# Weight sums of a seven-product down-projection: from loads and VectorE subtractions in the up-projection to accumulating DMAs beside the input projection

## The chip, the cores and the metric

The kernel runs on one core of a Trainium2 chip. The metric is the device time of one execution in microseconds (us). A profile is one execution of its own; its time is given beside the median of the timed runs.

## The reference

One hybrid decoder layer on 1024 tokens of width 1024, with 16 learned meta tokens put ahead (1040 rows in all). The input projection feeds four differential-attention heads and four HGRN2 heads side by side; their outputs are joined, projected and added to the residual; a gated FFN with a causal convolution of width 3 follows.

```python
a = rmsnorm(h, ln_mix_pre)
dq, dk, dv, hq, hf, hi, hg = split(a @ w_in)
mix = concat([diff_attention(dq, dk, dv, ...), hgrn2(hq, hf, hi, hg, ...)]) @ w_out
h = h + rmsnorm(mix, ln_mix_post)
a = rmsnorm(h, ln_ffn_pre)
u = causal_depthwise_conv(a @ w_up, conv_w, 3) + conv_b      # 1024 -> 2 x 2816
gate, up = split(u, 2)
y = (gelu(gate) * up) @ w_down                               # 2816 -> 1024
h = h + rmsnorm(y, ln_ffn_post)
return h[16:]
```

All inputs and outputs are float32.

## The kernel before

**Products.** Each float32 operand is split into a high part (a cast on ScalarE) and a low part (a subtraction on VectorE or POOL), both fp32r; each product is three matmuls (high by high, high by low, low by high). `split` does it, and `load_split` loads a tile first (SP issues nearly all DMAs).

**Input projection and heads.** `dense()` yields the projection of one tile of 128 columns after the other, each in three groups of rows (`proj_group`); while a tile is being multiplied the next one's weights are loaded and split. `interleave` mixes its steps with those of a head: the tiles of HGRN head h with attention head h, the tiles of attention head h+1 with HGRN head h. The loop over the four heads runs 25 tiles, 75 groups, through `dense`. Ahead of it, the attention's bias tables are made: `rb` tiles, partly cleared by POOL, are stored to DRAM (`rsc<-rb`). The first HGRN head's `f`, written by ScalarE, later takes over the place of the `rb` tiles. In each HGRN head POOL helps with products over halves of a tile (`tt<-t`).

**FFN up-projection.** The width of 2816 is cut into 22 blocks of 128 (`ft`), for gate and up side each. Both FFN projections use a seven-product scheme in place of eight (a Strassen type), in which sums of operand quarters are multiplied. Block 0 is done plainly (`plain_unit`); for each later block, `prep` makes seven split weight operands (`uh`, `ul`, from loads `ra` and sums `ws`), and `unit(ft, p)`, for the two halves p of the rows, does the seven products into three PSUM banks `pa`, `pb`, `pc`. Copies and additions between products write `x1` (`x<-pa`), `u2`, `u3` (`u<-pb,x`), and the outputs `ug`, `uu`. The fourth and the sixth product are added into `pb` again, so they have to wait until VectorE has read it. `gated` then does the convolution (`c`), gelu and product, and stores to the DRAM tensor `gsc`.

**Down-projection.** Its seven-product scheme needs four sums of quarters of the weight matrix, 1408 x 512 each. Before, `down_sums` in the up-projection makes them from block 6 (`SUMS`) on, at four of the seven steps of a block: per row tile k of 11, SP loads the four quarters into SBUF (`wd`, in the four "gk" buffers of the pool "down"), VectorE subtracts four times (`wd<-wd,wd`, 128 x 512), and SP stores the results to the DRAM tensor `tsc`. The tail then runs the products in `ORDER` 1, 2, 5, 6, 3, 7, 4, each over 11 row tiles: `operands` loads the gated activations (`gi<-gsc`, in "gk" buffers too, or the kept `ga`, `gb`, `gc`, `gs`) and the weights (`wi`, from `w_down` or `tsc`) and splits both into `gh`, `gl` and `wh`, `wl`; the matmuls go into `pd`.

**Order.** TensorE's instructions stand in the order in which the program is written. VectorE, ScalarE, POOL and SP get an order from the scheduler, which looks at when an instruction's inputs and its buffer are ready by its own costs; each engine then runs its list strictly in order, and so does SP with its DMAs. `issue_after` holds an instruction until another has been issued. All elementwise instructions pass through one helper, line 54.

Of the kernel before, what the change touches and what calls it, by code (L numbers as in the profile page):

```python
# [9 lines left out]
F32 = mybir.dt.float32  # L10
# [3 lines left out]
ALU = mybir.AluOpType  # L14
# [3 lines left out]
P = 128  # L18
# [6 lines left out]
NF = DFF // P  # L25
# [6 lines left out]
WN = [258, 256]  # L32
C0 = [0, 514]
FA, FH, FO = 840, 800, 740
SUMS = 6


def start(i):
# [21 lines left out]
def interleave(dense, sides, fill, lead=0):  # L60
    sides = list(sides)
    live = True

    def feed(budget):
        nonlocal live
        while live and budget > 0:
            c = next(dense, False)
            if c is False:
                live = False
            elif c is None:  # L70
                return
            else:
                budget -= c

    feed(lead)
    while sides:
        for s in list(sides):
            c = next(s, False)
            if c is False:
                sides.remove(s)  # L80
                continue
            feed(fill * (c or 1))
    feed(1e12)
# [3 lines left out]
def layer_kernel(ctx: ExitStack, tc: tile.TileContext, x, meta, table, lbl, gpre, gpost, win,  # L87
# [3 lines left out]
    V, A = Ordered(tc, nc.vector, state), Ordered(tc, nc.scalar, state)  # L91
    G = Ordered(tc, nc.gpsimd, state)
    T, SY = nc.tensor, nc.sync

    def pool(name, bufs, side="left", space=None):
        kw = {"side": side} if space is None else {"space": space}
        cm = tc.tile_pool(name=name, bufs=bufs, reuse_waits="tile", **kw)
        return cm, cm.__enter__()
# [35 lines left out]
    tsc = dp.tile([4, DFF // 2, 512], F32, tag="tsc", name="tsc")  # L134
# [47 lines left out]

    last_load = []

    at_p_cm, ap_ = pool("attn", 1, "right")
    z_cm, zp = pool("pre", 2, "right")

# [3 lines left out]
    def proj_group(g, parts, name, evac):  # L191
        b0, b1 = GROUPS[g]
        t0, t1 = start(b0), start(b1 - 1) + P
        n = t1 - t0
        pt = ps_in(f"pi_{name}_{g}")
        for k in range(KD):
            yield from proj_step(pt[:, :n], parts, k, t0, t1, lambda: evac(g, b0, b1, t0, t1, pt[:, :n]))
# [14 lines left out]
    gb = zp.tile([P, D], F32, tag="gb", name="gb", bufs=1)  # L212
# [121 lines left out]
    def carried():  # L334
        tails = list(carry)
        carry.clear()
        return tails
# [385 lines left out]
                yield from values(i + 1)  # L723
        carry.append(pend.pop("tail"))

    def dense(tiles, preload=None):
        parts = preload
        for idx, (m, name, evac) in enumerate(tiles):
            if parts is None:
                parts = load_m(m, name)  # L730
            nxt = load_m(tiles[idx + 1][0], tiles[idx + 1][1]) if idx + 1 < len(tiles) else None
            for g in range(3):
                for step, c in enumerate(proj_group(g, parts, name, evac)):
                    if step == 14:
                        flush()
                    yield c
            parts = nxt

    t_a, tiles = attn_in(0)
# [188 lines left out]

    for h in range(HEADS):
        t_h, tiles_h = hgrn_in(h)  # L930
        interleave(dense(tiles_h), [attn(h, t_a)] + carried(), FA, 1500)
        if h < HEADS - 1:
            t_a, tiles_a = attn_in(h + 1)
            interleave(dense(tiles_a), [hgrn_head(t_h)] + carried(), FH, 1500)

    close(at_cm)
    wo_cm, wop = pool("wo", 7)
# [283 lines left out]
    for i in range(1, NBLK):  # L1221
        py = ps_b(f"py1_{i}")
# [42 lines left out]
    marks = {}  # L1265
# [100 lines left out]
    dn_cm, dn = pool("down", 4, "right")  # L1366
    next(p0)
    for j in range(4, 7):
        prep(7 + j)

    def down_sums():
        for k in range(NF // 2):
            b = {}
            for nm, kk, half in (("11", k, 0), ("12", k, 1), ("22", k + NF // 2, 1), ("21", k + NF // 2, 0)):
                b[nm] = dn.tile([P, 512], F32, tag="gk", name=f"wd{nm}_{k}")
                SY.dma_start(b[nm], wdown[P * kk: P * (kk + 1), 512 * half: 512 * (half + 1)])
            yield
            for j, d, p_, q_ in ((0, "11", "12", "11"), (2, "12", "22", "12"), (1, "22", "22", "11"), (3, "21", "21", "22")):
                V.tensor_tensor(b[d], b[p_], b[q_], op=ALU.subtract)
                SY.dma_start(tsc[j][P * k: P * (k + 1)], b[d])  # L1380
                yield

    wd_sums = down_sums()
    for ft in range(1, NF):
        units = [unit(ft, p, ps_b) for p in range(2)]
        for j in range(7):
            prep(7 * (ft + 1) + j)
            for u in units:
                next(u)
            if ft >= SUMS and j in (1, 3, 5, 6):  # L1390
                with tc.issue_after(marks["last"].ins):
                    next(wd_sums, None)
            if (ft, j) == (1, 1):
                with tc.issue_after(marks[1, 1].ins):
                    next(p1)
# [31 lines left out]
    def sums5(k):  # L1427
        SY.dma_start(keep["gc"][:, k], g_src(k, 1))
        b = g_in(k + NH, 1, "5")
        V.tensor_tensor(keep["gs"][:, k], keep["gc"][:, k], b, op=ALU.add)  # L1430
        SY.dma_start(keep["ga"][:, k], g_src(k, 0))

    def operands(pr, k):
        ga, gb, gc, gs = (keep[nm][:, k] for nm in ("ga", "gb", "gc", "gs"))
        if pr == 1:
            a = g_in(k, 0, "1")
        elif pr == 2:
            SY.dma_start(gb, g_src(k + NH, 0))
            a = gb
        elif pr == 5:  # L1440
            a = gs
        elif pr == 6:
            V.tensor_tensor(gs, gs, ga, op=ALU.subtract)
            a = gs
        elif pr == 3:
            V.tensor_tensor(gb, gb, gs, op=ALU.subtract)
            a = gb
        elif pr == 7:
            V.tensor_tensor(ga, ga, gc, op=ALU.subtract)
            a = ga  # L1450
        else:
            a = g_in(k + NH, 1, "4")
        b = w_in(pr, k)
        nm = f"{pr}_{k}"
        gh = dn.tile([P, 512], F32R, tag="gh", name=f"gh{nm}")
        gl = dn.tile([P, 512], F32R, tag="gl", name=f"gl{nm}")
        split(gh, gl, a, V)
        wh = wp.tile([P, 512], F32R, tag="wh", name=f"wh{nm}", bufs=4)
        wl = wp.tile([P, 512], F32R, tag="wl", name=f"wl{nm}", bufs=4)
        split(wh, wl, b, V)  # L1460
        return gh, gl, wh, wl
# [41 lines left out]
    def evac(pr, m, py):  # L1503
        if pr == 1:
            A.copy(x1[:, m], py)
        elif pr == 2:
            V.tensor_tensor(c11[:, m], py, x1[:, m], op=ALU.add)
            squares(c11[:, m], m, 0)
            as_bias(m, 0)
            G.tensor_tensor(c11[:, m], c11[:, m], gfo[:, :512], op=ALU.mult)  # L1510
        elif pr == 5:
            A.copy(x5[:, m], py)
        elif pr == 6:
            V.tensor_tensor(u2[:, m], py, x1[:, m], op=ALU.add)
        elif pr == 3:
            c = u2[:, m]
            V.tensor_tensor(c, py, c, op=ALU.add)
            squares(c, m, 1)
            s_ = rstd(m, 1)
            hh = fp.tile([P, D], F32, tag="hh", name=f"hh{m}", bufs=2)  # L1520
            SY.dma_start(hh, hsc[P * m: P * (m + 1), :])
            V.scalar_tensor_tensor(hh[:, :512], c11[:, m], s_, hh[:, :512], ALU.mult, ALU.add)
            G.tensor_tensor(c, c, gfo[:, 512:], op=ALU.mult)
            V.scalar_tensor_tensor(hh[:, 512:], c, s_, hh[:, 512:], ALU.mult, ALU.add)
            SY.dma_start(out[P * m: P * (m + 1), :], hh)
        elif pr == 7:
            V.tensor_tensor(x1[:, m], py, x1[:, m], op=ALU.add)
            c = x5[:, m]
            V.tensor_tensor(c, c, x1[:, m], op=ALU.add)
            squares(c, 4 + m, 1)  # L1530
            as_bias(4 + m, 1)
            G.tensor_tensor(c, c, gfo[:, 512:], op=ALU.mult)
        else:
            c = x1[:, m]
            V.tensor_tensor(c, py, c, op=ALU.add)
            squares(c, 4 + m, 0)
            V.tensor_tensor(c, c, gfo[:, :512], op=ALU.mult)
            s_ = rstd(4 + m, 0)
            hh = hhs[m]
            V.scalar_tensor_tensor(hh[:, :512], c, s_, hh[:, :512], ALU.mult, ALU.add)  # L1540
            if m == 3:
                V.scalar_tensor_tensor(hh[:, 512:], x5[:, m], s_, hh[:, 512:], ALU.mult, ALU.add)
            else:
                A.mul(x5[:, m], x5[:, m], s_)
                G.tensor_tensor(hh[:, 512:], hh[:, 512:], x5[:, m], op=ALU.add)
            SY.dma_start(out[P * (4 + m): P * (5 + m), :], hh)
# [91 lines left out]
```

## Time and profile before

| | |
|---|---|
| median of three runs | 1334.59 us (1334.57 to 1335.59) |
| profiled execution | 1334.41 us |
| its span | 1332.6 us |
| mean granted TensorE clock | 0.995 |
| TensorE busy | 1288.0 us, 97% |
| VectorE, ScalarE, POOL busy | 931.6, 692.5, 456.2 us |
| DMA engines, mean busy share | 38%, 165 MB |
| FFN up-projection, blocks 2 to 21 | 694.6 to 1106.1 us |

In the profile, PE is TensorE, PEld its weight loads, DVE is VectorE, ACT ScalarE, POOL GpSimd and SP SyncE, whose queue issues the DMAs. A row of the timeline gives start, duration, engine, line, operation, output and inputs, shapes, and in brackets how long the engine stood before it and for what. A row of a group gives count, busy time in us and the mean of one in ns, then the idle time before. A row of the waits gives the waiting and the awaited instruction, then us in total, times, and the longest. A row cut by windows gives the stretch, its length, and the busy time and count of PE, PEld, DVE, ACT and POOL, then the granted clock, the DMA share and GB/s. A row of the DMA issues gives count, KB each, and the median time to landing.

### The profile page before, as it was taken

Reading aid. Unit: us, or ns where it says so; the run is one execution under the profiler, and the core shown is the slowest. Engines: PE = TensorE matmul, PEld = TensorE weight load, DVE = VectorE, ACT = ScalarE, POOL = GpSimd, SP = SyncE. Lnnn points to the kernel's source line nnn. Section 1 sums busy time; section 2 is a strip of 40 time slices with the busy share of each in tenths; the row PEclk is TensorE's granted clock in tenths of the full one; section 3 lists DMA queues with packets and bytes.
Section 4 is the critical chain, followed back from the end, with each engine's and each line's share of the span. In section 5 each row is a group of like instructions: output and inputs, shape, how many; then the busy total and the mean of one; then the engine's idle time right before and its main releaser. Section 6 shows DMA issues by size and latency. Waiting matters only on the chain.

```text
span 1332.6 us, 26191 instructions
## 1 busy us (share of the span) xinstructions
PE 1288.0 (97%) x10172; PEld 1187.6 (89%) x10172; DVE 931.6 (70%) x1531; ACT 692.5 (52%) x1635; POOL 456.2 (34%) x340
## 2 busy tenths in 40 slices
PE   8999999999999999899999999999999989999997
PEld 7899999899999988677999999999999988878875
DVE  6464646465645664547997788988989886697586
ACT  8465466447544755246754444444444444454553
POOL 5211211121112110344076667677676630010121
PEclk9999999999999999999999999999999999999999
DMA  6111111112111234587232224545445436955363
GB/s 208 61 41 32 54 56 41 48 45 64 44 41 33 88 100 152 170 265 265 83 111 80 80 96 152 181 147 163 162 147 170 156 120 214 329 176 166 88 205 119
DMA packets 99427, 165.00 MB, mean 124 GB/s; under 512 B 10035, under 2 KB 34899, under 8 KB 99302
## 3 DMA queue, kind: packets, MB, share of 16 engines
q1 hardware_dynamic: 99302, 163.32, 37.8%
q8 instruction: 80, 1.31, 0.4%
q14 instruction: 45, 0.37, 0.1%
HBM read 122.65 MB, written 40.63 MB: 123 GB/s over the span
## 4 chain that ended last, share of the span: by engine, by line
PE 43%; DVE 10%; DMA 4%; issue 3%; ACT 3%; POOL 1%; SPq 0%; DVEq 0%; ACTq 0%; POOLq 0%
PE pd L1484 5%; PE pd L1483 5%; PE pd L1485 5%; PE pb L1316 4%; DVE c L54 3%; PE pb L1317 3%; PE pb L1318 3%; PE pa L1316 2%; PE pa L1317 2%; PE pa L1318 2%; PE pc L1316 2%; PE pc L1317 2%; PE pc L1318 2%; DMA gi<-gsc 1%; DVE ul L54 1%
## 5 line engine op out<-in xcount | busy, mean ns | idle before, releaser
L1316 PE MATMUL pb<-t,uh 128*128 128x258 f32 x504 | 144.8, 287 | 11.9 <-DVE u L54 11.8
L1317 PE MATMUL pb<-t,uh 128*128 128x258 f32 x504 | 142.3, 282 | 0.0
L1318 PE MATMUL pb<-t,ul 128*128 128x258 f32 x504 | 142.3, 282 | 0.0
L1484 PE MATMUL pd<-wl,gh 128*128 128x512 f32 x308 | 122.0, 396 | 0.5 <-DVE wl L54 0.5
L1483 PE MATMUL pd<-wh,gh 128*128 128x512 f32 x308 | 121.7, 395 | 0.0
L1485 PE MATMUL pd<-wh,gl 128*128 128x512 f32 x308 | 121.7, 395 | 0.0
L54 POOL TENSOR_TENSOR c<-c,c 128x514 f32<-128x514 f32 (+1 forms) x44 | 74.9, 1702 | 120.6 <-ACT c L54 110.3
L1316 PEld LDWEIGHTS pb<-t,uh 128*128 128x128 f32 x504 | 96.1, 191 | 15.2 <-DVE u L54 15.0
L54 DVE SCALAR_TENSOR_TENSOR c<-uu,cwt,c 128x514 f32<-128x514 f32 (+1 forms) x88 | 87.6, 1004 | 22.6 <-ACT c L54 22.3
L1317 PEld LDWEIGHTS pb<-t,uh 128*128 128x128 f32 x504 | 96.3, 191 | 0.0
L1318 PEld LDWEIGHTS pb<-t,ul 128*128 128x128 f32 x504 | 95.9, 190 | 0.0
L1316 PE MATMUL pa<-t,uh 128*128 128x258 f32 (+1 forms) x336 | 95.2, 283 | 0.0
L1318 PE MATMUL pa<-t,ul 128*128 128x258 f32 (+1 forms) x336 | 95.0, 283 | 0.0
L1317 PE MATMUL pa<-t,uh 128*128 128x258 f32 (+1 forms) x336 | 94.8, 282 | 0.0
L1316 PE MATMUL pc<-t,uh 128*128 128x258 f32 (+1 forms) x336 | 94.4, 281 | 0.0
L1317 PE MATMUL pc<-t,uh 128*128 128x258 f32 (+1 forms) x336 | 94.0, 280 | 0.0
L1318 PE MATMUL pc<-t,ul 128*128 128x258 f32 (+1 forms) x336 | 93.7, 279 | 0.0
L54 DVE SCALAR_TENSOR_TENSOR c<-ug,cwt,c 128x514 f32<-128x514 f32 (+1 forms) x88 | 88.2, 1002 | 1.5 <-ACT c L54 1.4
L54 ACT CAST uh<-ra 128x512 fp32r<-128x512 f32 x67 | 41.0, 616 | 67.9 <-PE pb L1317 49.7
L54 POOL TENSOR_TENSOR ul<-ws,uh 128x512 fp32r<-128x512 f32 x42 | 63.8, 1519 | 27.1 <-ACT uh L54 27.1
L1484 PEld LDWEIGHTS pd<-wl,gh 128*128 128x128 f32 x308 | 57.7, 187 | 15.8 <-DVE wl L54 1.9
L1483 PEld LDWEIGHTS pd<-wh,gh 128*128 128x128 f32 x308 | 57.7, 187 | 14.1
(373 smaller groups left out, 4169.5 us busy)
## 6 DMA issues: line engine op xcount, KB each, us to landing
ra<-in_wup_dram SPq DMA_DIRECT2D x88, 256.0 KB, 3.0
mp<-msc SPq DMA_DIRECT2D x23, 512.0 KB, 5.5
wd<-in_wdown_dram SPq DMA_DIRECT2D x44, 256.0 KB, 3.3
tsc<-wd SPq DMA_DIRECT2D x44, 256.0 KB, 3.1
wi<-tsc SPq DMA_DIRECT2D x44, 256.0 KB, 2.8
gi<-gsc SPq DMA_DIRECT2D x33, 256.0 KB, 3.6
wi<-in_wdown_dram SPq DMA_DIRECT2D x33, 256.0 KB, 4.2
gsc<-c SPq DMA_DIRECT2D x22, 257.0 KB, 2.3
```

The source lines that it names most:

```text
L54: ins = call(*args, **kw)
L1316: T.matmul(pt, hi[:, s], th[:, k], start=(first and k == 0), stop=False, skip_group_check=True)
L1317: T.matmul(pt, hi[:, s], tl[:, k], start=False, stop=False, skip_group_check=True)
L1318: T.matmul(pt, lo[:, s], th[:, k], start=False, stop=(k == 3), skip_group_check=True)
L1483: T.matmul(py, gh[:, s], wh, start=(k == 0 and pr not in (3, 7)), stop=False, skip_group_check=True)
L1484: T.matmul(py, gh[:, s], wl, start=False, stop=False, skip_group_check=True)
L1485: T.matmul(py, gl[:, s], wh, start=False, stop=(k == NH - 1), skip_group_check=True)
```

## The change

The four weight sums are made wholly in DRAM. `down_sums` now sits ahead of the head loop and is a generator that `dense` advances once per projection group, for 55 steps. Per row tile k, SP copies four quarters of `w_down` into the four parts of `tsc`, DRAM to DRAM; then POOL issues four DMAs that add into these: parts 0 and 2 get a second quarter, part 3 gets part 1 (one row tile later), part 1 gets part 0. The adds are cut into pieces of 512 bytes, 128 elements each, by `max_dma_last_dim=512`. `issue_after` ties both to the latest weight load. [...] The loads, subtractions, stores and the `SUMS` of the up-projection are gone. In the scheduled order of the changed kernel TensorE's list is the same as before; the `gi` loads of the tail's first four row tiles, with their `gh` and `gl`, stand in blocks 1 to 4 of the up-projection, where they stood in the last blocks before.

```diff
--- before.py
+++ after.py
@@ -32,7 +32,6 @@
 WN = [258, 256]
 C0 = [0, 514]
 FA, FH, FO = 840, 800, 740
-SUMS = 6
 
 
 def start(i):
@@ -182,6 +181,33 @@
 
     last_load = []
 
+    def down_sums():
+        def quarter_of(k, r, c):
+            kk = k + NF // 2 * r
+            return wdown[P * kk: P * (kk + 1), 512 * c: 512 * (c + 1)]
+
+        def add(j, k, src):
+            with tc.issue_after(last_load[-1].ins):
+                G.dma_start(tsc[j][P * k: P * (k + 1)], src, accum_op=ALU.add, max_dma_last_dim=512)
+
+        for k in range(NF // 2 + 1):
+            if k < NF // 2:
+                for j, r, c in ((0, 0, 1), (2, 1, 1), (1, 1, 1), (3, 1, 0)):
+                    with tc.issue_after(last_load[-1].ins):
+                        SY.dma_start(tsc[j][P * k: P * (k + 1)], quarter_of(k, r, c))
+                yield
+                add(0, k, quarter_of(k, 0, 0))
+                yield
+                add(2, k, quarter_of(k, 0, 1))
+                yield
+            if k:
+                add(3, k - 1, tsc[1][P * (k - 1): P * k])
+                yield
+            if k < NF // 2:
+                add(1, k, tsc[0][P * k: P * (k + 1)])
+                yield
+
+    wd_sums = down_sums()
     at_p_cm, ap_ = pool("attn", 1, "right")
     z_cm, zp = pool("pre", 2, "right")
 
@@ -723,13 +749,14 @@
                 yield from values(i + 1)
         carry.append(pend.pop("tail"))
 
-    def dense(tiles, preload=None):
+    def dense(tiles, preload=None, side=iter(())):
         parts = preload
         for idx, (m, name, evac) in enumerate(tiles):
             if parts is None:
                 parts = load_m(m, name)
             nxt = load_m(tiles[idx + 1][0], tiles[idx + 1][1]) if idx + 1 < len(tiles) else None
             for g in range(3):
+                next(side, None)
                 for step, c in enumerate(proj_group(g, parts, name, evac)):
                     if step == 14:
                         flush()
@@ -928,10 +955,10 @@
 
     for h in range(HEADS):
         t_h, tiles_h = hgrn_in(h)
-        interleave(dense(tiles_h), [attn(h, t_a)] + carried(), FA, 1500)
+        interleave(dense(tiles_h, None, wd_sums), [attn(h, t_a)] + carried(), FA, 1500)
         if h < HEADS - 1:
             t_a, tiles_a = attn_in(h + 1)
-            interleave(dense(tiles_a), [hgrn_head(t_h)] + carried(), FH, 1500)
+            interleave(dense(tiles_a, None, wd_sums), [hgrn_head(t_h)] + carried(), FH, 1500)
 
     close(at_cm)
     wo_cm, wop = pool("wo", 7)
@@ -1367,29 +1394,12 @@
     next(p0)
     for j in range(4, 7):
         prep(7 + j)
-
-    def down_sums():
-        for k in range(NF // 2):
-            b = {}
-            for nm, kk, half in (("11", k, 0), ("12", k, 1), ("22", k + NF // 2, 1), ("21", k + NF // 2, 0)):
-                b[nm] = dn.tile([P, 512], F32, tag="gk", name=f"wd{nm}_{k}")
-                SY.dma_start(b[nm], wdown[P * kk: P * (kk + 1), 512 * half: 512 * (half + 1)])
-            yield
-            for j, d, p_, q_ in ((0, "11", "12", "11"), (2, "12", "22", "12"), (1, "22", "22", "11"), (3, "21", "21", "22")):
-                V.tensor_tensor(b[d], b[p_], b[q_], op=ALU.subtract)
-                SY.dma_start(tsc[j][P * k: P * (k + 1)], b[d])
-                yield
-
-    wd_sums = down_sums()
     for ft in range(1, NF):
         units = [unit(ft, p, ps_b) for p in range(2)]
         for j in range(7):
             prep(7 * (ft + 1) + j)
             for u in units:
                 next(u)
-            if ft >= SUMS and j in (1, 3, 5, 6):
-                with tc.issue_after(marks["last"].ins):
-                    next(wd_sums, None)
             if (ft, j) == (1, 1):
                 with tc.issue_after(marks[1, 1].ins):
                     next(p1)
@@ -1427,7 +1437,7 @@
     def sums5(k):
         SY.dma_start(keep["gc"][:, k], g_src(k, 1))
         b = g_in(k + NH, 1, "5")
-        V.tensor_tensor(keep["gs"][:, k], keep["gc"][:, k], b, op=ALU.add)
+        V.tensor_tensor(keep["gs"][:, k], b, keep["gc"][:, k], op=ALU.subtract)
         SY.dma_start(keep["ga"][:, k], g_src(k, 0))
 
     def operands(pr, k):
@@ -1440,13 +1450,13 @@
         elif pr == 5:
             a = gs
         elif pr == 6:
-            V.tensor_tensor(gs, gs, ga, op=ALU.subtract)
+            V.tensor_tensor(gs, gs, ga, op=ALU.add)
             a = gs
         elif pr == 3:
-            V.tensor_tensor(gb, gb, gs, op=ALU.subtract)
+            V.tensor_tensor(gb, gs, gb, op=ALU.subtract)
             a = gb
         elif pr == 7:
-            V.tensor_tensor(ga, ga, gc, op=ALU.subtract)
+            V.tensor_tensor(ga, gc, ga, op=ALU.subtract)
             a = ga
         else:
             a = g_in(k + NH, 1, "4")
...
         elif pr == 6:
-            V.tensor_tensor(u2[:, m], py, x1[:, m], op=ALU.add)
+            V.tensor_tensor(u2[:, m], py, x1[:, m], op=ALU.subtract)
         elif pr == 3:
             c = u2[:, m]
-            V.tensor_tensor(c, py, c, op=ALU.add)
+            V.tensor_tensor(c, c, py, op=ALU.subtract)
...
         elif pr == 7:
-            V.tensor_tensor(x1[:, m], py, x1[:, m], op=ALU.add)
+            V.tensor_tensor(x1[:, m], py, x1[:, m], op=ALU.subtract)
             c = x5[:, m]
-            V.tensor_tensor(c, c, x1[:, m], op=ALU.add)
+            V.tensor_tensor(c, x1[:, m], c, op=ALU.subtract)
...
             c = x1[:, m]
-            V.tensor_tensor(c, py, c, op=ALU.add)
+            V.tensor_tensor(c, py, c, op=ALU.subtract)
```

## The prediction

> **What bounds the kernel now.** I read the page's shares first, then the chain that ended last, then what TensorE waited for.
>
> ```profile
> span 1332.6 us, 26191 instructions
> PE 1288.0 (97%) x10172; PEld 1187.6 (89%) x10172; DVE 931.6 (70%) x1531; ACT 692.5 (52%) x1635; POOL 456.2 (34%) x340
> ...
> PE 43%; DVE 10%; DMA 4%; issue 3%; ACT 3%; POOL 1%; SPq 0%; DVEq 0%; ACTq 0%; POOLq 0%
> ...
> PE pb L1316 <- DVE u L54: 9.3, 11, 3.5
> ```
>
> TensorE is busy for 97% of the span, and the change does not touch its instructions, so the most that can be won is the 3% in which it stands, and what it loses to a slow clock. The last row is TensorE's waits from 770 to 1110 us, the FFN's up-projection with the sums: 9.3 us in 11 waits for one thing, VectorE's read of the `pb` bank (`u2`, `u3`) before the next product may be added into it. To see what the sums cost I cut the up-projection at the start of a block (`x<-pa`): blocks 2 to 6 without sums, 7 to 18 with them, 19 to 21 and the rest of block 21.
>
> ```profile
> core 0: us, PE busy (x) PEld busy (x) DVE busy (x) ACT busy (x) POOL busy (x), PEclk, DMA share, GB/s
> 694.58:794.03 99.45, 99.45 (x839) 99.36 (x838) 76.05 (x113) 48.00 (x87) 64.78 (x45) 1.00 0.25 83
> 794.03:1042.24 248.21, 242.36 (x2017) 240.00 (x2017) 222.10 (x304) 113.45 (x206) 173.84 (x108) 1.00 0.49 159
> 1042.24:1106.09 63.85, 60.34 (x492) 59.83 (x491) 49.19 (x75) 28.48 (x52) 25.62 (x17) 0.97 0.39 127
> ...
> L54 DVE TENSOR_TENSOR wd<-wd,wd 128x512 f32<-128x512 f32 x44 | 51.1, 1161 | 0.0
> ```
>
> In the first stretch TensorE has no gap (99.45 of 99.45) and a block takes 99.45/5 = 19.89 us. In the second VectorE is busy for 222.10 of 248.21 us (89%, against 76% before) and a block takes 248.21/12 = 20.68 us; its 44 subtractions `wd` (mean 1161 ns) are the main thing that the first stretch lacks.
>
> **Part 1: the sums leave the up-projection.** Removed: 44 loads, 44 subtractions, 44 stores. What matters on the path is the excess of the second and third stretch over the free pace. Blocks 7 to 18: 248.21 − 12 × 19.89 = 9.5 us. Blocks 19 to 21 have 492 TensorE instructions, of 2017/12 = 168 a block, so 2.93 blocks: 63.85 − 2.93 × 19.89 = 5.6 us. Sum **−15.1**. The instructions of block 7 on then stand on VectorE in the order that blocks 4 and 5 have now, and these have no gap, so nothing else is late next. The floor of this term is −9.3 (the waits alone), the ceiling −15.1 and what a smaller DMA load might add. The 88 issues that SP loses pay nothing, as SP is idle between them.
>
> **Part 2: what moves in their place.** The tail's operands for its first product (`gi`, split into `gh` on ScalarE and `gl` on VectorE) use the same "gk" buffers as the `wd` tiles. With these gone the buffers are free from the start: the instruction order of the changed kernel has `gi_0` to `gi_3` behind the `gsc` stores of blocks 0 to 3, and `gh`, `gl` of each in the middle of blocks 1 to 4, instead of blocks 19 and 20. What such a move does is already seen once, at the tail:
>
> ```profile
> 1053.01 0.32 SPq L1415 DMA_DIRECT2D gi<-gsc  x1
> ...
> 1056.38 0.62 ACT L54 CAST gh<-gi 128x512 fp32r<-128x512 f32 x1 [3.45 <-DMA gi<-gsc]
> ...
> 1072.84 1.72 DVE L54 TENSOR_TENSOR gl<-gi,gh 128x512 fp32r<-128x512 f32 x1
> ...
> 1072.97 0.39 PE L1316 MATMUL pb<-t,uh 128*128 128x258 f32 x1 [3.47 <-DVE u L54]
> ...
> 1074.10:1077.30 3.20, 3.20 (x16) 3.08 (x16) 3.20 (x4) 0.00 (x0) 3.12 (x2) 0.50 0.60 189
> ```
>
> An engine that reaches such a copy stands until the load has landed (3.45 us on ScalarE, with a load issued 3.35 us earlier). And after TensorE's gap of 3.47 us its granted clock is 0.50 over the whole of 1074.10 to 1077.30: 16 matmuls where the full clock would have done some 32, so about 1.7 us lost beside the gap. Block 1 now:
>
> ```profile
> 687.40 0.33 SPq L1284 DMA_DIRECT2D gsc<-c  x1
> 699.50 2.91 SPq L1284 DMA_DIRECT2D gsc<-c  x2
> 718.96 2.91 SPq L1284 DMA_DIRECT2D gsc<-c  x2
> 739.35 2.92 SPq L1284 DMA_DIRECT2D gsc<-c  x2
> ...
> 687.73 1.44 DVE L54 TENSOR_TENSOR ul<-ra,uh 128x512 fp32r<-128x512 f32 x1
> 689.09 0.41 DVE L54 TENSOR_TENSOR uu<-pb,x 128x258 f32<-128x258 f32 x1
> 690.45 0.76 DVE L54 SCALAR_TENSOR_TENSOR c<-uu,cwt,c 128x514 f32<-128x514 f32 x1 [0.95 <-ACT c L54]
> 696.97 0.69 DVE L54 TENSOR_TENSOR ul<-ra,uh 128x512 fp32r<-128x512 f32 x1
> 700.55 0.74 DVE L54 TENSOR_TENSOR u<-pb,x 128x258 f32<-128x258 f32 x2
> ...
> 701.02 0.39 PE L1316 MATMUL pb<-t,uh 128*128 128x258 f32 x1
> ```
>
> Block 0's last store is issued at 687.40 to 687.73; `gi_0` goes out right behind and lands some 3.1 us later, at 690.9. `gh_0` (0.62) ends at 691.5, `gl_0` (0.69, as the `ul` at 696.97, which has the same shape) at 692.1, and the `ul` that now starts at 687.73 follows, so `uu_0` starts at 692.75 instead of 689.09: VectorE is late by 3.65 us. From there to 700.55 it runs all but without a pause (one wait of 0.95, for ScalarE's copy of that same `uu`), so `u2` of block 2, at 700.55, and the matmul behind it, at 701.02, are 3.65 late: **+3.65**, and, as the gap is as long as that of 3.47, a half-clock spell of **+1.7**. In blocks 2 to 4 `gl_k` stands ahead of `u3_0`, which product 5 waits for. By the second store of each pair (issued at the end of its row), a load of 3.1 and 0.62 for `gh`, between 0.69 and 1.57 for `gl`, and 0.41 for `u3`, that is ready at about 727.0 in block 3 and 747.4 in block 4, some 0.3 and 0.7 us behind TensorE's present pace; in block 2 TensorE is late already: **+1.0**. Sum +6.35. Bounds: +3, if the stall of block 1 falls under 2.5 us and no spell follows; +18, if each of blocks 2 to 4 stands for 2.5 us and has a spell too (5.35 + 3 × 4.2).
>
> **Part 3: the DMAs beside the input projection.** Added: 44 copies DRAM to DRAM on SP and 44 accumulating DMAs issued by POOL, one step ahead of each of the first 55 projection groups. POOL takes its instructions in order: the second row's add waits until the first row's add has landed, and the add of the third row until the second's, so POOL stands at these. Behind them stand the last `rb` memset and the halving trees.
>
> ```profile
> 56.67 0.21 POOL L54 MEMSET rb<- 128x128 f32 x1 [0.25 <-DVE rb L54]
> 58.10 0.33 SPq L308 DMA_DIRECT2D rsc<-rb  x1
> 65.19 0.43 ACT L54 ACTIVATE f<-kr 128x272 f32<-128x272 f32 x1
> 147.14 0.40 POOL L54 TENSOR_TENSOR tt<-t 128x130 f32<-128x130 f32 x1 [11.38 <-DVE hq L54]
> 152.11 0.70 DVE L54 TENSOR_TENSOR kr<-kr,tt 128x520 f32<-128x520 f32 x1
> ...
> wr_hi<-in_win_dram SPq DMA_DIRECT2D x8, 256.0 KB, 2.6
> X_in<-in_win_dram SPq DMA_DIRECT2D x3, 256.0 KB, 7.3
> rsc<-rb SPq DMA_DIRECT2D x4, 192.0 KB, 2.5
> ```
>
> `f` takes over the place of `rb` in SBUF and so waits for the last `rsc` store. To keep 65.19 the memset must start by 65.19 − 2.5 − 0.21 = 62.5. The first add can go at about 52, when its copy is there. With L from an add's start to its landing and c for POOL's own time per issue, the memset comes free at 52 + 2L + c. No row of before shows either. For L I take a load, a store and an issue, 2.6 + 2.5 + 0.33 ≈ 5.5 (bounds: 2.6, one transfer alone, and 7.3 + 2.5 ≈ 10). For c I take four times SP's 0.33, as the rows are cut into four pieces, 1.3 (bounds 0.33, and 4, three POOL passes of 1.3 us). `f` is then late by 2 × 5.5 + 1.3 − 10.5 = 1.8 us; as TensorE has little slack there I count 1.5 of it. The trees have 152.11 − 147.5 = 4.6 us of slack, and POOL is free for 11.4 us ahead of them, which four issues of 1.3 do not fill: 0. For 44 issues on SP's queue and the traffic 0.5. Sum **+2.0** (0 to +16).
>
> By the Trainium skill's page "DMA: Bandwidth & Descriptors", section "Anatomy of one DMA — SWDGE (gpsimd) path", a DMA issued by GpSimd takes 2.0 us and its bytes by 436e3, by which I estimate 2.6 us for 262,144 bytes. By that `f` is not late, and the sum would be 1.5 us lower. No run here shows it.
>
> **Part 4: turned signs.** The tail's subtractions and sums are as many, on the same engine, with the same operands: 0.
>
> **Sum.** −15.1 + 6.35 + 2.0 = −6.75 on the profiled execution's own 1334.41 us (span 1332.6; the median of the three is 1334.59, 0.2 above), so **1327.7 us**. A difference of 0.2%, 2.7 us, is about what a measurement of this kernel can tell from none.
>
> **Rivals.**
> *The waits of the moved split are hidden.* If `gi_0` lands within 1 us of need, part 2 is +1 and part 3 +1: 1321 to 1324. Against it: the load follows the store directly, and the tail's load took 3.35 us. Chance 0.10.
> *More spells.* If two of blocks 2 to 4 stand for 2.5 us and have a spell each, part 2 is 5.35 + 2 × (2.5 + 1.7) = 13.75 and the time 1334.41 − 15.1 + 13.75 + 2.0 = 1335.1 (1332 to 1337). The loads would have to take 2 us more than the 3.35 of the row. Chance 0.15, no change.
> *POOL held by its own adds* (slower). With L = 10 and c = 4 the memset is late by 2 × 10 + 4 − 10.5 = 13.5 us, and each of the first two heads' trees stands behind four issues of 4 us, which the order puts some 10 us ahead of it: 16 − 10 − 4.6 of slack, 1.5 late. Sum +16.5 in place of +2.0, so 1334.41 − 15.1 + 6.35 + 16.5 = 1342.2. It turns the sign where part 3 passes 8.75 us: 2L + c above 19. For it: nothing in the profile bounds a DMA issued by POOL, and VectorE is busy beside it. Against: L has to be twice a load and a store. Chance 0.22.
> The Trainium skill's page "SBUF — State Buffer", section "Who interferes with whom", has VectorE and GpSimd share one pair of ports, and GpSimd's descriptor making held up while VectorE holds it. By that rule c would grow where VectorE's work is thick, which is this rival's way; the `wd` mean of 1161 ns against 690 for like shapes agrees with the shared pair, but no run here shows it for descriptors.
> *The change does not free TensorE.* If something other than VectorE's load held blocks 7 to 18 (DMA share 0.49 against 0.25 is the other difference), the gain is under 5 and the time 1336 to 1343. Against it: all 11 waits name VectorE. Chance 0.03.
>
> **How the numbers follow.** The forecast case (1324 to 1332) has 0.50. Faster by over 0.2%, below 1331.9: 0.50 + 0.10 = 0.60. Within 0.2%: the 0.15 of the spells. Slower: 0.22 + 0.03 = 0.25. The range leaves out half of the slower rival at its top and a part of the low rival at its bottom: 1322 to 1342; the forecast's own is 1324 to 1332.
>
> **What would show it.** Right: blocks 7 to 21 at 19.9 us each; a gap of about 3.6 us before product 3 of block 2, then a clock of 0.50; `f` at 66 to 68 us; POOL's wait between two adds about 5.5 us. Wrong: gaps in blocks 7 to 18 that remain; `f` beyond 72 or trees late in heads 0 and 1; spells in blocks 3 and 4.

## The result, and the profile after

The changed kernel takes 1340.68 us, the median of 14 runs (1334.29 to 1346.87), against 1334.46 us (1332.09 to 1337.94) for the kernel before in as many: a ratio of 1.0049, 95% interval 1.0033 to 1.0066. It is slower by 6.2 us, where 6.75 us less were forecast. Its runs also spread over 12.6 us, those of before over 5.9. The profiled execution took 1338.79 us, with a span of 1337.0.

The page of the changed kernel:

```profile
span 1337.0 us, 26124 instructions
PE 1287.5 (96%) x10172; PEld 1188.6 (89%) x10172; DVE 896.1 (67%) x1487; ACT 693.1 (52%) x1635; POOL 482.9 (36%) x384
...
PE 48%; DVE 7%; ACT 3%; issue 2%; DMA 2%; POOL 1%; SPq 0%; DVEq 0%; POOLq 0%; ACTq 0%
...
tsc<-in_wdown_dram SPq DMA_DIRECT2D x44, 256.0 KB, 4.6
tsc<-in_wdown_dram POOLq DMA_DIRECT2D x22, 256.0 KB, 6.4
```

TensorE has the same 10172 matmuls in the same order, so the two traces can be laid side by side, matmul for matmul, and the difference of their start times read off. It grows and shrinks in three places: +12.1 us up to the out-projection's end, of which +10.1 come at once near 70 us; then +7.2 us in blocks 2 to 4 of the up-projection; then −14.8 us from block 7 to the first product of the down-projection. Sum +4.5; the two profiled executions differ by 4.4.

The projection and the heads: three rows of TensorE's waits (45 to 560 us) and two of POOL's (45 to 360 us) in the changed kernel, then the timeline of POOL around the largest wait, with SP's store, ScalarE's `f` and the stretch of TensorE behind the wait:

```profile
PE pa L720 <- ACT az L53: 8.2, 1, 8.2
PE pl L449 <- DVE hq L53: 2.6, 2, 1.6
PE pa L720 <- DVE at L53: 1.6, 1, 1.6
...
POOL tsc L53 <- DMA tsc<-in_wdown_dram: 54.1, 22, 4.7
POOL tsc L53 <- DMA tsc<-tsc: 27.4, 6, 7.9
```

```profile
52.80 1.47 POOL L53 DMA_DIRECT2D tsc<-in_wdown_dram  x1 [1.60 <-PE pi_dk L233]
...
55.16 1.77 POOL L53 DMA_DIRECT2D tsc<-in_wdown_dram  x1
59.52 1.05 POOL L53 DMA_DIRECT2D tsc<-tsc  x1 [2.59 <-DMA wr_hi<-in_win_dram]
...
69.78 1.03 POOL L53 DMA_DIRECT2D tsc<-tsc  x1 [7.91 <-DMA tsc<-tsc]
70.45 0.58 POOL L53 MEMSET rb<- 128x128 f32 x1
...
71.05 0.33 SPq L334 DMA_DIRECT2D rsc<-rb  x1
...
75.39 0.43 ACT L53 ACTIVATE f<-kr 128x272 f32<-128x272 f32 x1 [10.23 <-DMA wr_hg<-in_win_dram]
...
77.78:81.50 3.72, 3.71 (x13) 3.62 (x14) 2.98 (x12) 2.25 (x9) 1.06 (x1) 0.51 0.67 75
```

The wait of 8.2 us on `az` is new. POOL issues the first add at 52.80, stands until it has landed, issues the dependent one at 59.52, and stands again until that has landed: the third of the chain goes out at 69.78. Only then comes the last `rb` memset, at 70.45 instead of 56.67. Its store lands at 75.24, and `f`, at 65.19 before, starts at 75.39. (The releaser that the row names, a weight load, is the one that the profile saw last; the run with the memset moved, below, shows which it was.) The waiting matmul starts 8.35 us later than in the kernel before; the rest of the 10.1 us, 1.75, is lost behind it, where the granted clock is 0.51 from 77.78 to 81.50. Over all, POOL stands for 81.5 us at copies and adds that have not landed.

The wait of 1.6 us is new too. It comes at 217 us, behind an add and two splits that POOL runs back to back after a wait (the row names a matmul as what ended it):

```profile
209.56 1.02 POOL L53 DMA_DIRECT2D tsc<-tsc  x1 [4.29 <-PE pi_hf L231]
210.23 2.89 POOL L53 TENSOR_TENSOR wl_hi<-wr_hi,wh_hi 128x512 fp32r<-128x512 f32 x2
210.74 2.54 DVE L53 TENSOR_TENSOR ona<-ona,nssa 16x128 f32<-16x128 f32 x1
...
216.98 0.49 PE L720 MATMUL pa<-avn,az 128*128 128x128 f32 x2 [1.57 <-DVE at L53]
```

VectorE's `ona`, 128 elements a row, takes 2.54 us and ends within 0.2 us of POOL's second split; the copy `at` that the matmul waits for stands behind it on VectorE. The 634 VectorE instructions from 45 us to the end of this stretch (577 us; 565 in the kernel before) are busy for 301.0 us against 289.2.

The up-projection of the changed kernel by stretches (blocks 1 to 6, 7 to 18, the rest, and 3.65 us behind a gap), then the timeline of block 1 on SP, ScalarE and VectorE with the matmul that waits for it:

```profile
683.19:813.22 130.03, 122.40 (x1010) 121.41 (x1009) 100.35 (x140) 62.47 (x110) 83.94 (x57) 0.99 0.27 86
813.22:1052.42 239.20, 239.20 (x2018) 239.20 (x2017) 181.00 (x265) 115.47 (x204) 153.99 (x108) 1.00 0.26 85
1052.42:1110.60 58.18, 58.18 (x492) 58.18 (x491) 40.88 (x66) 26.61 (x47) 23.64 (x17) 1.00 0.23 78
...
716.55:720.20 3.65, 3.65 (x19) 3.65 (x20) 1.11 (x2) 0.70 (x2) 3.57 (x3) 0.57 0.45 142
```

```profile
699.89 0.38 SPq L1425 DMA_DIRECT2D gi<-gsc  x1
702.76 0.62 ACT L53 CAST gh<-gi 128x512 fp32r<-128x512 f32 x1 [5.32 <-DMA gi<-gsc]
703.42 0.69 DVE L53 TENSOR_TENSOR gl<-gi,gh 128x512 fp32r<-128x512 f32 x1 [3.53 <-ACT gh L53]
716.55 0.58 PE L1343 MATMUL pb<-t,uh 128*128 128x258 f32 x1 [3.36 <-DVE u L53]
```

Blocks 7 to 18 take 239.20 us without a gap, against 248.21; the rest 58.18 against 63.85: 14.7 us are won. In block 1 ScalarE and VectorE stand at `gi_0`, TensorE at VectorE's `u2` for 3.36 us, and the granted clock is 0.57 behind that.

### The profile page after: what moved, and what is told of

Same layout as the page of the kernel before. It is cut to its first block, busy times and chain, and to the rows that moved or that the text cites. A ratio compares the mean times of both kernels' runs of the same rounds, so it can differ in the third digit from the quotient of the medians.

```text
span 1337.0 us, 26124 instructions
## 1 busy us (share of the span) xinstructions
PE 1287.5 (96%) x10172; PEld 1188.6 (89%) x10172; DVE 896.1 (67%) x1487; ACT 693.1 (52%) x1635; POOL 482.9 (36%) x384
## 4 chain that ended last, share of the span: by engine, by line
PE 48%; DVE 7%; ACT 3%; issue 2%; DMA 2%; POOL 1%; SPq 0%; DVEq 0%; POOLq 0%; ACTq 0%
PE pd L1494 5%; PE pd L1495 5%; PE pd L1493 5%; PE pb L1343 4%; PE pb L1344 4%; PE pb L1345 4%; PE pa L1343 3%; PE pa L1345 3%; PE pa L1344 3%; PE pc L1343 2%; PE pc L1344 2%; PE pc L1345 2%; PE py L1003 2%; PE py L1001 1%; PE py L999 1%
## 5 line engine op out<-in xcount | busy, mean ns | idle before, releaser
L53 DVE SCALAR_TENSOR_TENSOR c<-uu,cwt,c 128x514 f32<-128x514 f32 (+1 forms) x88 | 97.1, 1104 | 20.6 <-ACT c L53 19.9
L53 POOL TENSOR_TENSOR c<-c,c 128x514 f32<-128x514 f32 (+1 forms) x44 | 63.4, 1440 | 122.7 <-ACT c L53 120.0
L53 POOL TENSOR_TENSOR ul<-ws,uh 128x512 fp32r<-128x512 f32 x42 | 60.5, 1440 | 43.0 <-ACT uh L53 38.2
L1495 PEld LDWEIGHTS pd<-wh,gl 128*128 128x128 f32 x308 | 57.7, 187 | 13.9
```

The costliest lines, as they stand in the source:

```text
L53: ins = call(*args, **kw)
L1495: T.matmul(py, gl[:, s], wh, start=False, stop=(k == NH - 1), skip_group_check=True)
```

## The experiments

Two theories on the 12.1 us: A, POOL, in order, is held at adds that have not landed, and holds what is queued behind it; B, the added traffic and SP's queue slow the projection's own loads and stores.

**Adds started later.** `dense` advances the generator from the fourth group on.

```diff
+    skip = iter(range(3))
...
-                next(side, None)
+                if next(skip, None) is None:
+                    next(side, None)
```

> The changed kernel with the generator of copies and adds started three projection groups later, behind head 0's first tile, so that the last rb memset stands ahead of every add on POOL. Theory A (POOL, in order, is held at its dependent adds, and the rb memset and f with it): of the 12.1 us lost up to the up-projection the 10.1 at 65 to 78 us go, 2 to 4 remain, time about 1331. Theory B (the traffic of copies and adds slows the projection's own loads and stores): the loss only moves, 8 to 12 us remain, time 1337 or more.

1334.0 us (1328.29 to 1340.29), ratio to before 0.9996 (0.998 to 1.0011), same as before, where theory A expected 1331 and theory B 1337 or more. `f` starts at 65.16, and the 10.1 us are gone. But 9.1 us come up later, from 230 us on, in steps of up to 2.2 us with slow clock behind some of them, so the loss is not at `rb` alone: by this run alone it has moved, as theory B had it. One such step, VectorE's `nssa` before, then the same instruction here with what POOL does meanwhile, and the matmul that waits for VectorE's copy `at`, four instructions on:

```profile
228.47 0.16 DVE L54 SCALAR_TENSOR_TENSOR nssa<-nssa 128x3 f32<-128x3 f32 x1
```

```profile
228.67 3.30 DVE L53 SCALAR_TENSOR_TENSOR nssa<-nssa 128x3 f32<-128x3 f32 x1
228.37 1.03 POOL L53 DMA_DIRECT2D tsc<-tsc  x1 [3.66 <-DMA tsc<-tsc]
229.01 2.92 POOL L53 TENSOR_TENSOR wl_hg<-wr_hg,wh_hg 128x512 fp32r<-128x512 f32 x2
234.57 0.50 PE L640 MATMUL E<-k,q 128*128 128x512 f32 x1 [1.84 <-DVE at L53]
```

An operation on three elements a row takes 3.30 us instead of 0.16: it begins while POOL, released from its wait, runs an add and two splits back to back, and ends as the last of them ends, at 231.9. From 236 to 239 us the granted clock is 0.50. The same 634 VectorE instructions are busy for 299.1 us in this run.

**Copies only.** The adds are left out.

> The changed kernel with the 44 adds left out; the copies stay, so the four sums hold one quarter each. Theory A (POOL held at its adds): f is at 65 to 67 us, the loss up to the up-projection falls from 12.1 to 0 to 2 us, time about 1330. Theory B (traffic and SP's queue): 6 us or more remain, time 1335 or more.

1325.76 us (1323.29 to 1326.12), ratio 0.9929 (0.9917 to 0.9941). `f` is at 65.20, and up to 490 us TensorE is never more than 0.2 us off the kernel before. 44 copies on SP cost nothing by themselves, so B falls as far as the copies go, and all of the 12 us belongs to the adds; whether it is the adds' traffic or POOL's wait, the run with the adds put off tells. By the medians the adds cost 14.9 us (1340.68 − 1325.76), more than the 12.1 of the profiled execution. Blocks 2 to 4 lose 6.3 us here, and the 14.8 us won behind them are as in the changed kernel.

**The memset moved.** `G.memset(rb...)` becomes `V.memset(rb...)`; the adds stand where they did.

> The changed kernel with the four rb memsets moved from POOL to VectorE; copies and adds stand where they did. Theory A (the loss at 65 to 78 us is the memset behind POOL's held adds): f is at 65 to 68 us, 2 to 4 us of the 12.1 remain, time about 1331. Theory B (traffic, which delays the rsc store itself and the weights): f is late by 5 us or more all the same, time 1336 or more.

1336.0 us (1331.81 to 1344.75), ratio 1.0013 (0.9997 to 1.003). `f` starts at 68.15 instead of 75.39, and TensorE is 1.6 us late at 75 us, not 10.1. So it was the memset behind POOL's waits, for this step. The total misses the 1331 that was expected by theory A, by the steps that follow: 9.9 us are lost by 490 us in the profiled execution, which is the fastest of the twelve.

**The adds put off.** Each add goes one round of steps later than what it reads, and behind the latest weight split of POOL.

```diff
-            with tc.issue_after(last_load[-1].ins):
+            with tc.issue_after(last_lo_[-1].ins):
                 G.dma_start(tsc[j][P * k: P * (k + 1)], src, accum_op=ALU.add, max_dma_last_dim=512)
...
+            if has(k - 1):
+                add(0, k - 1, quarter_of(k - 1, 0, 0))
...
+            if has(k - 2):
+                add(1, k - 2, tsc[0][P * (k - 2): P * (k - 1)])
...
+            if has(k - 3):
+                add(3, k - 3, tsc[1][P * (k - 3): P * (k - 2)])
```

> The changed kernel with each add put off until what it reads landed a round of steps earlier (parts 0 and 2 one round behind the copies, part 1 two, part 3 three), and tied behind the latest weight split on POOL; as many copies and adds as before. Theory A (POOL's waits at unlanded adds cost the time, by themselves and by the run of POOL instructions that is left behind them and holds VectorE's small operations): the loss up to the up-projection falls from 12.1 to 0 to 2 us, time about 1330, and the spread of the runs closes. Theory C (the adds' own issue, 1.0 to 1.3 us each on POOL, holds VectorE wherever it falls): 3 to 6 us remain, with a spread of several us, time about 1333.

1325.04 us (1323.69 to 1326.35), ratio 0.9928 (0.9916 to 0.994): the time of the kernel without adds, and its spread. No row of POOL's waits names a copy or an add as what an add waits for any more; ahead of adds POOL stands for 12.1 us in six places with no releaser shown, against the 81.5 us. TensorE is never more than 0.2 us off the kernel before up to 490 us, and VectorE's 634 instructions are busy for 291.0 us. The issues take what they took, or more, as POOL's rows by tile show:

```profile
L53 POOL DMA_DIRECT2D tsc<-in_wdown_dram x22: 1224/1379/2258, 56.4 to 347.2; - x22
L53 POOL DMA_DIRECT2D tsc<-tsc x22: 1016/1082/2110, 96.4 to 406.1; - x22
```

(minimum, median and maximum in ns). 44 issues of 1.0 to 1.4 us and as many landings of 5 to 7 us cost nothing where nothing waits, so theory C falls. The traffic of copies and adds is all there, so what was left of theory B falls too. The edit does two things at once, the delay and the new place behind the splits; no run separates them. Blocks 2 to 4 lose 9.1 us in this profiled execution.

**Adds uncut.** `max_dma_last_dim` goes from 512 to 2048 bytes.

> The changed kernel with the adds' rows of 2048 bytes left whole instead of cut into four pieces of 512. If POOL's issue time goes by the pieces, as the prediction took it, an issue falls from 1.0 to 1.3 us to some 0.4 to 0.6 us and a landing from 4.6 to 6.4 us to some 4 us; the first tile's loss then falls from 10.1 to some 5 us, time about 1335. If the issue has a fixed cost and the landing goes by the queue, both stay and the time stays at 1340.

1339.57 us (1335.35 to 1345.93), ratio 1.0043 (1.0023 to 1.0064), the changed kernel's time. An issue falls to 0.81 us (median), the landings hardly: 5.9 and 4.3 us against 6.4 and 4.6. By an estimate from these times (a quarter of the pieces saves 0.24 to 0.49 us), the issue has a fixed part of some 0.7 us and the pieces are the lesser part. POOL stands for 108.6 us at copies and adds here: the landing is what it waits for.

**The splits held back.** `gh` and `gl` of the early `gi` wait for `x1` and `u2` of three blocks later.

```diff
-        split(gh, gl, a, V)
+        if pr == 1 and k < 4:
+            with tc.issue_after(marks["x", k + 3, 0].ins), tc.issue_after(marks[k + 3, 0].ins):
+                split(gh, gl, a, V)
+        else:
+            split(gh, gl, a, V)
```

> The changed kernel with the splits gh and gl of the four early gi loads held back on ScalarE and VectorE to three blocks after their load, behind x1 and u2 of blocks 3 to 6; the loads stay. Theory (the 7.2 us lost in blocks 2 to 4 are the engines' stand at loads not yet landed): these go and nothing comes in their place, time about 1340.7 - 7.2 = 1333.5. Rival (VectorE is late wherever the split stands): 4 to 7 us remain in blocks 3 to 6, time about 1339.

1335.51 us (1333.19 to 1342.28), ratio 1.001 (0.9998 to 1.0023). Blocks 1 to 6 lose nothing against the kernel before, blocks 7 on win the same 14.8 us. The difference to the changed kernel is 5.2 us, with the adds' spread still on it. Without adds it can be read more closely:

> Copies without adds (the sums hold one quarter each), with the splits of the four early gi loads held three blocks behind their loads: the floor of this change if adds cost nothing. Copies alone took 1325.8; the stand in blocks 1 to 4 was 6.1 us of that. Expected 1319.7. Rival (VectorE is late wherever the splits stand): 1323 or more.

1317.79 us (1317.04 to 1319.66), ratio 0.9876 (0.9863 to 0.9888). By the ratios that is 0.53%, 7.1 us, less than the copies alone (by the medians 8.0), where the stand was 6.3 us in the profiled execution. The remainder is within what the intervals leave open.

**Both edits.**

> Both edits: adds put off as in the run before, and the splits of the four early gi loads held three blocks behind their loads. The parts should add: the time of the run before less 6 us. By theory A about 1322 to 1324, by theory C about 1327. It should beat the kernel before by 0.5 to 0.9%.

1317.74 us (1315.31 to 1321.52), ratio 0.9876 (0.986 to 0.9891): 1.2% faster than the kernel before and level with the kernel that has no adds at all. Against the run with the adds put off alone it wins 7.3 us by the medians, where 6 were expected.

**What the up-projection's loss was.** Two runs on the kernel before. First its subtractions are cut to one column, so that only VectorE is relieved:

```diff
-                V.tensor_tensor(b[d], b[p_], b[q_], op=ALU.subtract)
+                V.tensor_tensor(b[d][:, :1], b[p_][:, :1], b[q_][:, :1], op=ALU.subtract)
```

> The kernel before with its 44 subtractions cut to one column each (the sums are wrong in the other 511): all loads, stores and waits of the sums stay, and VectorE is relieved of about 40 us. Theory (blocks 7 to 18 lost 9.5 us to VectorE's load): these go and, as the tail's gi splits stay in the last blocks, the 5.6 us of blocks 19 to 21 mostly stay, time about 1334.5 - 9.5 = 1325. Rival (the DMA traffic of the sums, share 0.49 against 0.25): 5 us or more of the 9.5 stay, time 1330 or more.

```profile
793.63:1034.65 241.02, 240.72 (x2020) 239.84 (x2019) 197.60 (x303) 114.63 (x205) 156.11 (x108) 1.00 0.50 163
```

1326.23 us, ratio 0.9935 (0.9919 to 0.9952). Blocks 7 to 18 take 241.02 us with the DMA share still 0.50: 7.2 of the 9.0 us were VectorE's load. Then the sums stay and the tail's four splits go to blocks 20 and 21 (the edit above with `20 + k // 2` for `k + 3`):

> The kernel before, its sums untouched, with the splits of the first four gi loads held to blocks 20 and 21 (behind x1 and u2 there), about one block after their loads. Theory (the 5.6 us of blocks 19 to 21 are the engines' stand at loads that have not landed, with its half-clock spell): about 4 to 5 us go, time about 1330. Rival (VectorE is late at the end for all its work, wherever these four splits stand): time within 1 us of 1334.5.

1328.95 us, ratio 0.9952 (0.9938 to 0.9967). The steps near 1073 us shrink by 4.2 us in the profiled execution, by 5.8 in the medians: the last blocks' loss was for the most part these splits. VectorE's subtractions had no share in it: with them cut to one column TensorE loses in these blocks what it lost before, within 0.2 us. The remaining 1.5 us of the 5.7 are not explained.

## Why the prediction was wrong, point by point

**Part 1 held.** −15.1 was forecast, −14.7 (by stretches) to −14.8 measured, its two pieces 9.0 and 5.7 against 9.5 and 5.6. The reason given was right for the first piece. The second was for the most part (4.2 us) the tail's own `gi` splits and not the sums: it went because the change moves these splits, a reason that part 1 does not give, so that the right size of this piece is in good part luck.

**Part 2 held in its mechanism.** `gi_0` at 699.89 is 687.83 in the time of before (12.06 us of shift), forecast 687.73; VectorE is late by 3.5 us (forecast 3.65), TensorE's gap is 3.36, and gap and slow clock together cost 4.84 (forecast 5.35). The difference is mostly the spell: the prediction's 16 matmuls in 3.20 us would have taken 1.9 us at the pace of its first stretch (99.45/839 us each), not 1.6, so its row gives a loss of 1.3 us and not 1.7; measured are 4.84 − 3.36 = 1.5. Blocks 2 to 4 lose 2.4 us, not 1.0, as one gap of 1.79 comes in block 4, which the estimate of 0.7 was too small for. Sum 7.2 against 6.35.

**Part 3 failed: +12.1 us in the profiled execution, 14.9 by the medians, where +2.0 was the term.** The step that failed for 10.1 of these is the landing L of the first adds, taken as 5.5 us for both. The first add does land 6.4 us after its issue (52.80 to 59.23), near the estimate; the second of the chain takes 9.9 us (59.52 to 69.44), the bound and not the value taken. POOL issued another add between the two, which lands at 65.91, and eight copies of 256 KB are issued from 48.6 to 60.0 us, the last four of them while these adds run; two of these four have a landing in the trace, 7.25 and 9.67 us after their issue. In the run with the adds started later, where no copy is issued between 57.3 and 75.4 us, the first two of the chain land in 6.5 and 4.2 us, on average 5.4, near the 5.5 that was taken. This points to the next row's copies beside the adds, for which part 3 had only 0.5 us; no run shows it by itself. So 2L + c is 6.4 + 9.9 + 1.0 = 17.3 in place of 12.3; the first add goes at 52.8 and not at 52, and the `rsc` store lands 4.2 us after its issue (71.05 to 75.24) where 2.5 was taken. `f` is late by 10.2 instead of 1.8; at 75.39 it is beyond the 72 that the prediction named as a sign of being wrong. TensorE's slack was larger than the 0.3 counted (10.2 − 8.35 = 1.85 us), but the slow clock behind the gap, which part 2 counted and part 3 did not, took 1.75 back. The issue time c was right: 1.0 to 1.3 us against 1.3. The formula for the memset was right as well, and the slower rival has its mechanism (POOL held by its own adds), for 12.1 us in the profiled execution and 14.9 by the medians against its 16.5. It did not need L = 10 twice, c = 4 or the late trees; 2L + c was 17.3 and the sign turned below the 19 that the prediction set, for the store, the slow clock and the steps that follow add to it.

**What was put at nothing.** The other few us in part 3 come where POOL's wait ends, and where the first 10.1 are taken away they grow to 8 to 10 (the runs with the adds later and with the memset moved). The prediction had looked for the trees, which were not late enough to matter, and not for VectorE, whose small operations stretch while the run of POOL instructions lasts that has piled up behind a wait (0.16 to 3.30 us). By the Trainium skill's page "SBUF — State Buffer", section "Who interferes with whom", a VectorE instruction with two inputs in SBUF contends with a GpSimd instruction that reads SBUF. The trace agrees in that `ona` and `nssa`, both with two inputs in SBUF, end within 0.2 us of POOL's second split (213.1 and 231.9 us); that the ports are the reason is not shown by a run. The prediction set the shared pair beside c, the time of an issue, which did not grow.

**Part 4 held.** The four sums are made by adding alone, and the tail's signs turn with that; from the first product of the down-projection to the end TensorE's shift changes by 0.15 us, where 0 was forecast.

**The size of the total.** The profiled execution shows +4.4, the medians +6.2. What the adds cost differs from run to run: up to the up-projection 12.1 us in the changed kernel's profiled execution, 16.7 in that of the run with the splits held back, whose adds stand the same. The spread of 12.6 us falls to 2.7, in five runs, when the adds are put off. So the forecast was wrong by part 3 alone: parts 1 and 2 together gave −7.6 us where −8.75 was forecast.

The Trainium skill's page "DMA: Bandwidth & Descriptors", section "Anatomy of one DMA — SWDGE (gpsimd) path", gives 2.0 us and the bytes by 436e3 for a DMA issued by GpSimd, an estimate of 2.6 us for these; the adds' median is 4.6 and 6.4 us, and the measurement decides.

## What to carry to other kernels

What the adds cost POOL here was not their issue but the wait for what they read: count for each DMA that a compute engine issues what it must see landed, and put it so far behind that this is long over. A landing taken from one transfer by itself is too short when the same change puts other transfers beside it. Taking away the one wait that a trace shows largest need not win its length; here the loss came up at the next places. Work that is taken away frees buffers, and a scheduler may use them to pull later work forward; look in the new order for what has moved into the middle of other work, and at whether its data will be there. A stage that carries slack before the change need not have it in the order that the change brings.

## What the runs showed of the hardware

A DRAM-to-DRAM add of 256 KB issued by POOL took 1.0 to 1.3 us of POOL and 4.6 to 6.4 us to land (medians of the changed kernel), up to 10.7 with another add ahead of it and copies beside it; 44 of them were free in the run in which POOL no longer waited for them. A VectorE instruction of 0.16 us lasted 3.30 us while POOL ran three instructions back to back. A gap of 3.36 us on TensorE was followed by a granted clock of 0.57 over 3.65 us, one of 8.2 us by 0.51 over 3.72 us. The prediction's bounds let a spell follow a gap of 2.5 us or more. One of 1.79 us was not followed by one (1.00 from 765.88 to 769.50 us), but one of 1.84 us was (before 234.57 us in the run with the adds started later: 0.50 from 236 to 239 us). These runs give no sure limit.
